# Making part of the low halves of split weights by an accumulating DMA in a two-layer decoder step

## The chip, the cores and the metric

The kernel runs on one core of one Trainium2 chip. The metric is the device time of one execution in microseconds, the median of several runs; lower is better.

## The reference, cut to what matters

The reference is one inference step of a two-layer decoder for 512 prompt tokens and 8 sample tokens that share the weights. Each layer is a half-step SwiGLU feed-forward network (FFN), a token mixer and a second FFN, each followed by a residual and a layernorm:

```python
def _swiglu(x, wg, wu, wd):
    return (jax.nn.silu(x @ wg) * (x @ wu)) @ wd

x = _layernorm(ALPHA * x + 0.5 * _swiglu(x, wg1, wu1, wd1), ...)
x = _layernorm(ALPHA * x + _mixer(x, ...), ...)
x = _layernorm(ALPHA * x + 0.5 * _swiglu(x, wg2, wu2, wd2), ...)
```

The model width is 1024, the FFN width 2816. The mixer has one input projection, three branches (windowed attention, a Mamba-2 scan, an HGRN2 scan), three gated branch projections and an output projection. All of it is float32. The multiplications by weights are most of the arithmetic, and the change concerns how a weight is made ready for them.

## The kernel before, in words

All 520 tokens stay on the chip, features on the 128 partitions and tokens along the free dimension, in two halves of 260 tokens. Weights are read from HBM in **units**. A float32 product is made of three matmuls in the type fp32r: a value is split into a high part (a copy rounded to fp32r) and a low part (the value less its high part), and `gemm` (lines 165 to 178) and `product` (lines 373 to 384) add high times high, weight high times activation low, and weight low times activation high, in this order.

The class `Weights` (from line 50) keeps the list of units in the order in which they are used. A **plain unit** is 128 rows by up to 1024 columns, mostly 512 KB (`_emit`, lines 77 to 92): SP loads it into a raw buffer `ws` (line 87), ScalarE copies it to `wh` (line 90), VectorE subtracts `wh` from `ws` into `wl` (line 91). A **pair** (`_emit_pair`, lines 94 to 113) is a gate unit g and an up unit u of an FFN, from which seven block products in the manner of Strassen are made in place of eight: sums of blocks are formed in two further raw buffers pa and pb by VectorE (L102, L103) and GpSimd (L104, L105), and `_split` (lines 67 to 75; cast L73, subtraction L74) splits g, pb, pa and the second half of u: seven quarters of 512 columns. There are five buffers each of `ws`, `wh` and `wl`, and a single one for the narrow split of u. `get` hands out the next unit and emits two units more than that; the emission has the highest priority (`EARLY[0]`), so a unit is loaded and split as soon as buffers allow.

TensorE uses most units for both token halves. At the end of an FFN or mixer the last projection is run over all units for the first half and then, with the same units loaded again, for the second half (`halves_last`), and the next stage begins likewise (`halves_head`, and the first ten projections of the mixer), so that the layernorm of one half (`ln_end`, lines 204 to 232, among it GpSimd's L224, VectorE's L225 and ScalarE's L228) runs beside matmuls of the other. A unit used for one half only is called a half unit below. Per layer there are 191 plain units (48 in each FFN, 95 in the mixer) and 36 pairs. An FFN has 16 half units at its start and 16 at its end, a mixer 20 and 16.

The order of instructions on each engine is fixed when the program is built: a scheduler with a timing model plays the program through and picks by priority. Each engine then runs its own list in order and waits on semaphores. All DMAs are issued by SP; GpSimd issues none.

Of the kernel before, what the change touches and what calls it, by code (L numbers as in the profile page):

```python
# [11 lines left out]
F32 = mybir.dt.float32  # L12
# [3 lines left out]
AF = mybir.ActivationFunctionType  # L16
ALU = mybir.AluOpType
# [32 lines left out]
class Weights:  # L50
# [13 lines left out]
    def _raw(self):  # L64
        return self.pool.tile([P, 1024], F32, tag="ws", name="ws", bufs=5)

    def _split(self, s, n=1024):
        nc = self.nc
        tag, bufs = ("", 5) if n > 512 else ("2", 1)
        h, lo = (  # L70
            self.pool.tile([P, 1024 if n > 512 else 512], F32R, tag=t + tag, name=t, bufs=bufs) for t in ("wh", "wl")
        )
        nc.scalar.copy(h[:, :n], s[:, :n])  # L73
        nc.vector.tensor_tensor(lo[:, :n], s[:, :n], h[:, :n].bitcast(F32), op=ALU.subtract)  # L74
        return h, lo

    def _emit(self):
        nc = self.nc
        unit = self.units[len(self.tiles)]
        with self.tc.high_priority(offset=EARLY[0]):  # L80
            if len(unit) == 2:
                self.tiles.append(self._emit_pair(*unit))
                return
            ap, kt, cols = unit
            n = kt * cols
            s = self._raw()
            nc.sync.dma_start(s[:, :n], ap)

            h, lo = (self.pool.tile([P, 1024], F32R, tag=t, name=t, bufs=5) for t in ("wh", "wl"))
            nc.scalar.copy(h[:, :n], s[:, :n])  # L90
            nc.vector.tensor_tensor(lo[:, :n], s[:, :n], h[:, :n].bitcast(F32), op=ALU.subtract)  # L91
        self.tiles.append((h, lo, kt, cols))

    def _emit_pair(self, ap0, ap1):


        nc = self.nc
        g, u, pa, pb = (self._raw() for _ in range(4))
        a, b = slice(0, 512), slice(512, 1024)
        nc.sync.dma_start(g, ap0)  # L100
        nc.sync.dma_start(u, ap1)
        nc.vector.tensor_tensor(pa[:, a], g[:, a], u[:, a], op=ALU.add)  # L102
        nc.vector.tensor_tensor(pb[:, a], pa[:, a], u[:, b], op=ALU.add)  # L103
        nc.gpsimd.tensor_tensor(pb[:, b], pb[:, a], g[:, b], op=ALU.add)  # L104
        nc.gpsimd.tensor_tensor(pa[:, b], u[:, a], u[:, b], op=ALU.add)  # L105
        gs, bs, as_ = self._split(g), self._split(pb), self._split(pa)
        us = self._split(u[:, b], 512)
        half = lambda t, k: tuple(x[:, k * 512 : k * 512 + 512] for x in t)
        return {
            "11": half(gs, 0), "21": half(gs, 1), "22": half(us, 0),  # L110
            "P1": half(as_, 0), "P3": half(as_, 1), "P2": half(bs, 0), "P4": half(bs, 1),
        }
# [1379 lines left out]
```

## Time and profile before

| | |
|---|---|
| median of 3 runs | 2638.61 us (2634.75 to 2639.36) |
| the profiled execution | 2647.04 us |
| its span, first to last instruction | 2645.2 us |
| mean granted TensorE clock | 0.986 of full speed |
| TensorE matmul busy | 97% |
| VectorE, ScalarE, GpSimd busy | 74%, 47%, 25% |
| moved by DMA | 318.17 MB |

In the rows below, PE is TensorE's matmuls and PEld its weight loads, DVE is VectorE, ACT ScalarE, POOL GpSimd, SP the engine that issues DMAs; a q behind an engine's name is its instruction queue. L91 is line 91 of the kernel. An entry like `wl<-ws,wh` names the tile that is written and those that are read.

### The profile page before, as it was taken

Reading aid. Unit: us, or ns where it says so; the run is one execution under the profiler, and the core shown is the slowest. Engines: PE = TensorE matmul, PEld = TensorE weight load, DVE = VectorE, ACT = ScalarE, POOL = GpSimd, SP = SyncE. Lnnn points to the kernel's source line nnn. Section 1 sums busy time; section 2 is a strip of 40 time slices with the busy share of each in tenths; the row PEclk is TensorE's granted clock in tenths of the full one; section 3 lists DMA queues with packets and bytes.
Section 4 is the critical chain, followed back from the end, with each engine's and each line's share of the span. In section 5 each row is a group of like instructions: output and inputs, shape, how many; then the busy total and the mean of one; then the engine's idle time right before and its main releaser. Section 6 shows DMA issues by size and latency. Waiting matters only on the chain.

```text
span 2645.2 us, 51891 instructions
## 1 busy us (share of the span) xinstructions
PE 2557.0 (97%) x20784; PEld 2486.7 (94%) x20784; DVE 1949.5 (74%) x3702; ACT 1250.3 (47%) x2358; POOL 667.8 (25%) x587
## 2 busy tenths in 40 slices
PE   8999999999899999999999999999998999999998
PEld 8999999898789999999989999999987899999997
DVE  8785888855485588868887868888544845988586
ACT  6342565543334473434663435754433344635355
POOL 2121243300033341212321122433000434312124
PEclk9999999999899999999999999999998999999999
DMA  6341457422442343232542414564224424332233
GB/s 206 109 131 62 143 165 218 142 67 77 86 137 90 114 150 99 92 114 81 189 132 86 136 65 148 185 191 137 81 73 75 144 83 134 122 112 92 101 115 126
DMA packets 159890, 318.17 MB, mean 120 GB/s; under 512 B 46788, under 2 KB 82340, under 8 KB 159648
## 3 DMA queue, kind: packets, MB, share of 16 engines
q1 hardware_dynamic: 159648, 314.86, 37.5%
q8 instruction: 163, 2.67, 0.4%
q14 instruction: 79, 0.65, 0.1%
HBM read 302.93 MB, written 11.88 MB: 119 GB/s over the span
## 4 chain that ended last, share of the span: by engine, by line
PE 70%; DVE 14%; DMA 8%; issue 3%; ACT 2%; POOL 2%; SPq 0%; ACTq 0%; POOLq 0%; DVEq 0%
PE g L176 14%; PE g L177 14%; PE g L178 14%; PE g L382 6%; PE g L384 6%; PE g L383 6%; DMA cb<-in_sconv 4%; DVE wl L91 3%; PE s L382 2%; PE s L383 2%; PE s L384 2%; DMA smp<-r8d 2%; DVE y L225 1%; PE s L1078 1%; DMA ws<-in_w_gu 1%
## 5 line engine op out<-in xcount | busy, mean ns | idle before, releaser
L176 PE MATMUL g<-xh,wh 128*128 128x260 f32 (+1 forms) x2336 | 676.6, 290 | 22.9 <-ACT cb L785 16.9
L178 PE MATMUL g<-xh,wl 128*128 128x260 f32 (+1 forms) x2336 | 674.6, 289 | 3.2 <-DVE wl L91 3.1
L177 PE MATMUL g<-xl,wh 128*128 128x260 f32 (+1 forms) x2336 | 674.6, 289 | 0.7 <-DVE xl L1356 0.7
L90 ACT CAST wh<-ws 128x1024 fp32r<-128x1024 f32 (+1 forms) x382 | 389.5, 1024 | 351.9 <-PE g L177 226.9
L91 DVE TENSOR_TENSOR wl<-ws,wh 128x1024 fp32r<-128x1024 f32 (+1 forms) x382 | 466.8, 1224 | 109.3 <-ACT wh L90 108.3
L176 PEld LDWEIGHTS g<-xh,wh 128*128 128x128 f32 (+1 forms) x2336 | 445.3, 191 | 34.8 <-ACT cb L785 18.7
L178 PEld LDWEIGHTS g<-xh,wl 128*128 128x128 f32 (+1 forms) x2336 | 444.9, 191 | 10.9 <-DVE wl L91 4.3
L177 PEld LDWEIGHTS g<-xl,wh 128*128 128x128 f32 (+1 forms) x2336 | 444.9, 190 | 8.7 <-issue 4.5
L73 ACT CAST wh<-ws 128x1024 fp32r<-128x1024 f32 (+1 forms) x288 | 265.3, 941 | 289.9 <-PE g L177 161.9
L178 PE MATMUL g<-hh,wl 128*128 128x260 f32 x1408 | 396.6, 283 | 0.0
L177 PE MATMUL g<-hl,wh 128*128 128x260 f32 x1408 | 395.9, 283 | 0.0
L176 PE MATMUL g<-hh,wh 128*128 128x260 f32 x1408 | 392.6, 283 | 1.5 <-DVE y L251 1.5
L74 DVE TENSOR_TENSOR wl<-ws,wh 128x1024 fp32r<-128x1024 f32 (+1 forms) x288 | 318.4, 1112 | 89.3 <-ACT wh L73 87.7
L105 POOL TENSOR_TENSOR ws<-ws 128x512 f32<-128x512 f32 x72 | 131.8, 1831 | 648.3 <-DMA ws<-in_w_gu 267.8
L176 PEld LDWEIGHTS g<-hh,wh 128*128 128x128 f32 x1408 | 263.4, 189 | 2.0 <-DVE y L251 1.9
L178 PEld LDWEIGHTS g<-hh,wl 128*128 128x128 f32 x1408 | 264.7, 188 | 0.2
L177 PEld LDWEIGHTS g<-hl,wh 128*128 128x128 f32 x1408 | 264.8, 188 | 0.1
L382 PE MATMUL g<-xh,wh 128*128 128x260 f32 x864 | 246.3, 286 | 2.0 <-ACT wh L73 1.6
L383 PE MATMUL g<-xl,wh 128*128 128x260 f32 x864 | 244.7, 284 | 0.0
L384 PE MATMUL g<-xh,wl 128*128 128x260 f32 x864 | 242.0, 283 | 0.0
L382 PEld LDWEIGHTS g<-xh,wh 128*128 128x128 f32 x864 | 163.9, 190 | 4.5 <-ACT wh L73 3.0
L382 PE MATMUL g<-sx,wh 128*128 128x260 f32 x576 | 163.7, 284 | 3.9 <-ACT wh L73 3.9
(404 smaller groups left out, 5701.3 us busy)
## 6 DMA issues: line engine op xcount, KB each, us to landing
ws<-in_w_gu SPq DMA_DIRECT2D x208, 512.0 KB, 3.3
ws<-in_w_in SPq DMA_DIRECT2D x132, 512.0 KB, 3.4
ws<-in_w_dn SPq DMA_DIRECT2D x96, 512.0 KB, 4.4
ws<-in_w_out SPq DMA_DIRECT2D x32, 512.0 KB, 3.9
ws<-in_w_dn SPq DMA_DIRECT2D x32, 384.0 KB, 3.1
smp<-r8d SPq DMA_DIRECT2D x48, 256.0 KB, 4.7
ws<-in_w_br SPq DMA_DIRECT2D x24, 512.0 KB, 4.5
smp<-in_hgr SPq DMA_DIRECT2D x16, 256.0 KB, 5.0
```

Of the source, the lines that this page charges most:

```text
L73: nc.scalar.copy(h[:, :n], s[:, :n])
L74: nc.vector.tensor_tensor(lo[:, :n], s[:, :n], h[:, :n].bitcast(F32), op=ALU.subtract)
L90: nc.scalar.copy(h[:, :n], s[:, :n])
L91: nc.vector.tensor_tensor(lo[:, :n], s[:, :n], h[:, :n].bitcast(F32), op=ALU.subtract)
L105: nc.gpsimd.tensor_tensor(pa[:, b], u[:, a], u[:, b], op=ALU.add)
L176: nc.tensor.matmul(out, lhsT=h[:, wc], rhs=xh[:, c0:c1], start=st, stop=False)
L177: nc.tensor.matmul(out, lhsT=h[:, wc], rhs=xl[:, c0:c1], start=False, stop=False)
L178: nc.tensor.matmul(out, lhsT=lo[:, wc], rhs=xh[:, c0:c1], start=False, stop=en)
L225: nc.vector.scalar_tensor_tensor(y, y, gn, rb, op0=ALU.mult, op1=ALU.mult)
L382: nc.tensor.matmul(out, lhsT=h[:, wc], rhs=xh, start=first and k == 0, stop=False, **go)
L383: nc.tensor.matmul(out, lhsT=h[:, wc], rhs=xl, start=False, stop=False, **go)
L384: nc.tensor.matmul(out, lhsT=lo[:, wc], rhs=xh, start=False, stop=k == HK - 1, **go)
```

## The change

A new helper `_parts` makes both parts of a split. With `dma` set, ScalarE still copies the high part and then writes the raw weights, negated and rounded to fp32r, into `lo`: the negated high part. GpSimd then issues a DMA that adds the raw weights to `lo`, which leaves the low part. Otherwise VectorE subtracts as before. The DMA is used for every second plain unit that is at least 512 columns wide, the first one included (the turn also passes at narrow units), and for g of each pair, two of its seven quarters. The sizes and numbers of buffers, the loads and the matmuls are the same.

```diff
--- before.py
+++ after.py
@@ -64,15 +64,24 @@
     def _raw(self):
         return self.pool.tile([P, 1024], F32, tag="ws", name="ws", bufs=5)
 
-    def _split(self, s, n=1024):
+    def _split(self, s, n=1024, dma=False):
+
         nc = self.nc
         tag, bufs = ("", 5) if n > 512 else ("2", 1)
         h, lo = (
             self.pool.tile([P, 1024 if n > 512 else 512], F32R, tag=t + tag, name=t, bufs=bufs) for t in ("wh", "wl")
         )
+        self._parts(h, lo, s, n, dma)
+        return h, lo
+
+    def _parts(self, h, lo, s, n, dma):
+        nc = self.nc
         nc.scalar.copy(h[:, :n], s[:, :n])
-        nc.vector.tensor_tensor(lo[:, :n], s[:, :n], h[:, :n].bitcast(F32), op=ALU.subtract)
-        return h, lo
+        if dma:
+            nc.scalar.activation(lo[:, :n], s[:, :n], AF.Copy, scale=-1.0)
+            nc.gpsimd.dma_start(lo[:, :n], s[:, :n], accum_op=ALU.add)
+        else:
+            nc.vector.tensor_tensor(lo[:, :n], s[:, :n], h[:, :n].bitcast(F32), op=ALU.subtract)
 
     def _emit(self):
         nc = self.nc
@@ -87,8 +96,8 @@
             nc.sync.dma_start(s[:, :n], ap)
 
             h, lo = (self.pool.tile([P, 1024], F32R, tag=t, name=t, bufs=5) for t in ("wh", "wl"))
-            nc.scalar.copy(h[:, :n], s[:, :n])
-            nc.vector.tensor_tensor(lo[:, :n], s[:, :n], h[:, :n].bitcast(F32), op=ALU.subtract)
+            self.turn = not getattr(self, "turn", False)
+            self._parts(h, lo, s, n, self.turn and n >= 512)
         self.tiles.append((h, lo, kt, cols))
 
     def _emit_pair(self, ap0, ap1):
@@ -103,7 +112,7 @@
         nc.vector.tensor_tensor(pb[:, a], pa[:, a], u[:, b], op=ALU.add)
         nc.gpsimd.tensor_tensor(pb[:, b], pb[:, a], g[:, b], op=ALU.add)
         nc.gpsimd.tensor_tensor(pa[:, b], u[:, a], u[:, b], op=ALU.add)
-        gs, bs, as_ = self._split(g), self._split(pb), self._split(pa)
+        gs, bs, as_ = self._split(g, dma=True), self._split(pb), self._split(pa)
         us = self._split(u[:, b], 512)
         half = lambda t, k: tuple(x[:, k * 512 : k * 512 + 512] for x in t)
         return {
```

## Rows read from the trace of the kernel before

**Rows 1.** The page, part 1: busy us, share of the span and instructions of each engine.
```profile
PE 2557.0 (97%) x20784; PEld 2486.7 (94%) x20784; DVE 1949.5 (74%) x3702; ACT 1250.3 (47%) x2358; POOL 667.8 (25%) x587
```

**Rows 2.** The page, part 4, by line: shares of the chain that ended last.
```profile
PE g L176 14%; PE g L177 14%; PE g L178 14%; PE g L382 6%; PE g L384 6%; PE g L383 6%; DMA cb<-in_sconv 4%; DVE wl L91 3%; PE s L382 2%; PE s L383 2%; PE s L384 2%; DMA smp<-r8d 2%; DVE y L225 1%; PE s L1078 1%; DMA ws<-in_w_gu 1%
```

**Rows 3.** Stretches of 53 us: us, busy (x instructions) by engine, PEclk, DMA share, GB/s.
```profile
0.00:53.00 53.00, 46.17 (x353) 45.28 (x354) 44.00 (x95) 37.48 (x68) 10.17 (x17) 1.00 0.68 236
...
371.00:424.00 53.00, 50.34 (x405) 49.70 (x404) 42.07 (x64) 38.21 (x64) 18.25 (x23) 0.97 0.56 184
...
954.00:1007.00 53.00, 48.10 (x379) 46.88 (x377) 48.69 (x85) 35.70 (x66) 17.13 (x17) 0.97 0.40 132
...
1007.00:1060.00 53.00, 52.86 (x426) 52.84 (x427) 43.64 (x73) 18.66 (x29) 8.75 (x6) 0.97 0.35 110
...
1272.00:1325.00 53.00, 51.59 (x427) 51.26 (x426) 45.81 (x69) 32.51 (x52) 24.29 (x22) 1.00 0.52 168
...
1325.00:1378.00 53.00, 48.64 (x391) 47.47 (x391) 49.12 (x83) 34.87 (x65) 16.07 (x16) 1.00 0.36 113
...
1643.00:1696.00 53.00, 50.47 (x415) 50.03 (x414) 45.85 (x66) 35.41 (x55) 27.10 (x26) 1.00 0.54 171
...
2226.00:2279.00 53.00, 50.40 (x401) 49.76 (x401) 43.74 (x65) 33.99 (x53) 30.13 (x28) 0.97 0.56 178
...
2279.00:2332.00 53.00, 50.75 (x406) 50.11 (x405) 49.59 (x83) 32.53 (x62) 13.15 (x11) 0.97 0.33 105
...
1166.00:1219.00 53.00, 53.00 (x445) 53.00 (x444) 31.66 (x49) 19.00 (x28) 9.73 (x7) 1.00 0.18 60
```

**Rows 4.** The same view of the four stretches with pairs.
```profile
106.00:318.00 212.00, 210.42 (x1744) 209.21 (x1743) 163.07 (x256) 89.91 (x145) 46.86 (x29) 1.00 0.30 98
...
1060.00:1272.00 212.00, 211.92 (x1760) 211.13 (x1759) 162.28 (x258) 91.57 (x148) 46.32 (x28) 1.00 0.32 108
...
1378.00:1643.00 265.00, 264.07 (x2192) 262.81 (x2191) 204.33 (x332) 110.25 (x176) 53.23 (x33) 1.00 0.34 112
...
2332.00:2597.00 265.00, 264.93 (x2201) 264.22 (x2200) 203.97 (x332) 111.34 (x179) 52.33 (x33) 1.00 0.33 108
```

**Rows 5.** Waits: idle us of the engine in total, times, longest us.
```profile
ACT wh L90 <- PE g L177: 226.9, 123, 6.2
```

**Rows 6.** Groups by line and shape: busy us, mean ns of one, idle before and its releasers.
```profile
L91 DVE TENSOR_TENSOR wl<-ws,wh 128x1024 fp32r<-128x1024 f32 x348 | 435.9, 1255 | 105.5 <-ACT wh L90 104.5
...
L74 DVE TENSOR_TENSOR wl<-ws,wh 128x1024 fp32r<-128x1024 f32 x216 | 264.4, 1226 | 74.2 <-ACT wh L73 72.6
...
L90 ACT CAST wh<-ws 128x1024 fp32r<-128x1024 f32 x348 | 362.7, 1046 | 303.6 <-PE g L177 209.9 <-PE g L383 37.8 <-issue 34.2
```

**Rows 7.** Line 105 alone: duration of one, ns, min/median/max.
```profile
L105 POOL TENSOR_TENSOR ws<-ws x72: 1280/1798/3575, 46.6 to 2565.7; 128x512 f32<-128x512 f32 x72
```

**Rows 8.** DMA queues and issues: share of 16 engines; count, KB, median us to landing.
```profile
q1 hardware_dynamic: 159648, 314.86, 37.5%
...
ws<-in_w_gu SPq DMA_DIRECT2D x208, 512.0 KB, 3.3
...
ws<-in_w_br SPq DMA_DIRECT2D x24, 512.0 KB, 4.5
...
smp<-in_hgr SPq DMA_DIRECT2D x16, 256.0 KB, 5.0
```

**Rows 9.** Timeline of one pair on ACT, POOL and SP: start us, us, instruction.
```profile
1228.35 1.05 ACT L73 CAST wh<-ws 128x1024 fp32r<-128x1024 f32 x1 [1.56 <-DMA ws<-in_w_gu]
...
1234.19 1.28 POOL L104 TENSOR_TENSOR ws<-ws 128x512 f32<-128x512 f32 x1 [2.39 <-DVE ws L103]
...
1235.51 0.33 SPq L100 DMA_DIRECT2D ws<-in_w_gu  x1
```

**Rows 10.** Timeline of the start on ACT and PE.
```profile
4.21 1.04 ACT L90 CAST wh<-ws 128x1024 fp32r<-128x1024 f32 x1 [2.20 <-DMA ws<-in_w_gu]
...
7.29 0.42 PE L178 MATMUL g<-xh,wl 128*128 128x260 f32 x1
```

## The prediction

> **What bounds the kernel now.** I read the page's engine busy times first: TensorE is busy for 97% of the span, VectorE for 74%, ScalarE for 47%, GpSimd for 25% [rows 1]. So the end is set by matmuls, and taking work from VectorE gains only where TensorE waits for it. The chain that ended last says how much that can be: matmuls fill it, and the subtraction of L91 holds 3% [rows 2], some 79 us of 2645.2, of which the change takes half at most.
>
> Where TensorE loses time is read from stretches of equal length [rows 3]. The stretch from 1166 us is a full one: 445 matmuls in 53 us, so a pitch of 0.119 us. The eight stretches listed at the ends of layers (last down projection, layernorm, first half units of the next stage) have 405, 379, 426, 427, 391, 415, 401 and 406: 310 too few, 36.9 us. In them VectorE is busy for 368.5 us of 424 (87%) and ScalarE for 261.9 (62%). In the four stretches with pairs [rows 4] 113 matmuls are missing of 954 us' worth, 13.5 us in all; there is little to win there.
>
> How early a weight unit is split follows from one wait: the cast of L90 sat idle 226.9 us, 123 times, until a matmul that read the high part had ended [rows 5]. The cast waits for one of five buffers, so the unit is made as soon as TensorE lets go of the unit five before: four units ahead. At the pitch above a half unit (24 matmuls) takes 2.86 us, a whole one 5.7 us, a pair (84 matmuls) 10.0 us. The lead is therefore 11.4 us among half units and 22.9 us among whole ones. There are 200 half units (32 in each of four FFNs, 36 in each of two mixers), in seven unbroken stretches.
>
> **The change, part by part.**
>
> *VectorE.* Of 382 plain units every second one moves; the two dt units are too narrow for it, and one of them has the turn, so 190 move, and with one a pair (72) that is 262 subtractions. At 1.255 and 1.226 us [rows 6] (16 of them are 768 wide and shorter) that is some 325 us less: 1949.5 becomes about 1625 us, 61%.
>
> *ScalarE.* 262 negated copies, bounded by the cast of the same shape at 1.046 us [rows 6], which is also the value I take: 274 us more, 1250 becomes 1524 us, 58%. In the eight stretches about half of some 115 plain units move: VectorE falls by about 70 us to 70%, ScalarE rises by 60 us to 76%. The fullest engine beside TensorE goes from 87% to 76%.
>
> *GpSimd.* 262 issues on its queue, which had no DMA. No row shows one. Below, nothing; above, 3.6 us, the longest of L105's additions; I take 1.3 us, the shortest of them [rows 7], since an issue moves no data through the engine. Each issue waits for the negated copy, and behind it stand L104, L105, and in a layernorm the subtractions of L224.
>
> *The DMAs.* No row shows one that reads and adds to what is there. Loads of 512 KB land 3.3 to 4.5 us after their issue, and one of 256 KB takes 5.0 [rows 8]. A load occupies the 16 engines for 37.5% of 2645.2 us over 314.86 MB, times 0.524 MB: 1.65 us [rows 8]. The accumulating one has to read twice as much, so I take 4.5 + 1.65, about 6 us; the ends are 3.3 us, as a plain load, and 10 us, as two slow transfers one after the other. By the Trainium skill, "DMA: Bandwidth & Descriptors", Anatomy of one DMA, a GpSimd-issued transfer takes 2.0 us plus its bytes at 436 GB/s; an estimate from that is 3.2 us, or 4.4 us with the second read, and with it the sum below would be about 3 us better, as no half unit would be late; no row here shows such a transfer.
>
> *The path of a moved unit.* Cast 1.05, negated copy 1.05, issue 1.3, landing 6: 9.4 us from the start of the cast, against 2.3 us and VectorE's queue now. Whole units have 22.9 us, so nothing is lost there. Half units have 11.4 us; 2.0 are to spare, and ScalarE's own queue takes some of that. I take +3 us over the seven stretches; the ends are 0 and, with a landing of 10 us, 2.0 us late. Every late unit holds up the next, so the lateness comes back once in six units (five for the buffer, one for the turn): 33 times 2.0, +67 us.
>
> *The eight stretches.* TensorE lost 36.9 us there. I take half of that back, -18 us, because the other half is the layernorm's own chain through all engines, which no load on VectorE explains. The ends are 0 and -25 us.
>
> *Pairs.* Only g moves, which is split before u has landed. Its cast begins at 1228.35, so its low part would be there at 1237.75 us. Until now g's raw buffer was last read by L104, ending at 1235.47, and SP issued the next g load at 1235.51 [rows 9]: that load goes out up to 2.2 us later, with u's load behind it on SP's queue. Against that stands 1.23 us taken from VectorE's queue in front of L102 and L103, which are next to be late. Net 1.0 us per pair at worst, and only once the stock of split weights is used up, near the end of a group of eight. I take +2 us for eight groups; the ends are -5 and +72 us (all 72 pairs).
>
> *Start.* The first unit of all has the turn: cast at about 4.2 us, low part at 13.6, and the first matmul with it now runs at 7.29 [rows 10]. That is 6.3 us late, less what can be run of other units' high parts meanwhile: +3 us, ends 0 and +6.3.
>
> *The convolution loads* in the mixer, 4% of the chain [rows 2], share the DMA engines: the added transfers occupy them for some 262 times 2 to 3.3 us, 20 to 33% more. Of this +1 us, ends 0 and +10.
>
> **The sum:** 3 - 18 + 2 + 3 + 1 = -9 us. The profiled execution took 2647.04 us (span 2645.2 and 1.8 around it), 8.4 us over the median of the runs, 2638.61; the difference is carried over to the median: 2630 us. About 5 us (0.2%) is what a measurement of this kernel can tell from no change.
>
> **Rivals.**
>
> *The transfer is too late among half units* (slower). The place is the first matmul with wl in the half-unit stretches, the price 33 us for each microsecond by which the path passes 11.4 us, and it decides from a landing of 8 us. For it: DMA engines are already busy for 0.33 to 0.68 of the time there [rows 3], and each half unit brings a load of its own. Against it: the loads there land in 3.3 to 4.5 us all the same. With a landing of 9 us to 9.5 us, 33 to 50 us late and 18 us gained: 2654 to 2671 us. Chance 0.27.
>
> *GpSimd becomes the queue that everything stands in* (slower). L105 takes 1.28 us alone and 1.80 in the median, 3.58 at most [rows 7]: GpSimd's work is stretched while VectorE runs. With issues of 3.6 us the path is 11.7 us, 0.3 late (10 us), and in each of six layer ends one issue stands in front of L224 (22 us); less 18 us gained that is +14: 2653 us. Chance 0.10. The Trainium skill, "SBUF — State Buffer", Who interferes with whom, has such a rule: GpSimd cannot write descriptors while VectorE runs in a two-port mode; it also says that two-input operations, which most here are, have no such mode.
>
> *Gain and loss cancel* (no change): if what TensorE loses at the layer ends is mostly the layernorm's chain, the relief gives 5 to 10 us and the other terms take 9: 2638 to 2643 us, about 2640. The chain's 3% for L91 speaks against it, the few waits of TensorE itself that end with wl for it. The order of all instructions is planned anew, which alone can move some microseconds either way. Chance 0.18. That the change does not do what it says I give nothing: the high part subtracted and the raw part added are the same numbers.
>
> **How the numbers follow.** The forecast's own case, relief worth more than lateness, has 0.45, with 2608 to 2633 us as its range. The slower cases have 0.37, the even one 0.18. The range goes from 2608 (25 us of relief and 5 in the pairs) to 2685 us, where a landing of almost 10 us ends less the relief; outside are the pairs' worst end and anything beyond.
>
> **What would show it.** L91 should stand at 192 and L74 at 216, a ScalarE group of 262 copies should appear, and 262 issues on GpSimd's queue with 5 to 7 us to landing. VectorE should fall to about 1625 us and ScalarE rise to about 1525. The eight stretches should hold some 150 matmuls more. The forecast is wrong if TensorE's waits name a DMA into wl among half units, if GpSimd's issues take 3 us or more, or if the pair stretches lose more than they do now.

## The result, and where the time went

The changed kernel takes 2919.67 us (median, 2915.28 to 2926.39) against 2638.99 us before: a ratio of 1.1069, 95% interval 1.1045 to 1.1094, so some 281 us slower. The profiled execution has a span of 2924.6 us. Its page, parts 1, 3, 5 and 6, with the lines that answer to [rows 1, 6, 8]:

```profile
span 2924.6 us, 52737 instructions
...
PE 2647.9 (91%) x20784; PEld 2552.3 (87%) x20784; DVE 1656.0 (57%) x3440; ACT 1481.4 (51%) x2620; POOL 801.1 (27%) x849
...
q1 hardware_dynamic: 159648, 314.86, 33.8%
q0 software_dynamic: 37728, 135.28, 24.4%
...
L187 PE MATMUL g<-xh,wl 128*128 128x260 f32 (+1 forms) x2336 | 694.6, 298 | 65.4 <-DMA wl<-ws 65.2
...
L84 DVE TENSOR_TENSOR wl<-ws,wh 128x1024 fp32r<-128x1024 f32 (+2 forms) x408 | 474.4, 1163 | 285.9 <-ACT wh L79 279.0
L82 POOL DMA_DIRECT2D wl<-ws x262 | 231.7, 884 | 1290.7 <-ACT wl L81 324.8
...
L187 PE MATMUL g<-hh,wl 128*128 128x260 f32 x1408 | 404.0, 289 | 45.3 <-DMA wl<-ws 45.3
...
L81 ACT ACTIVATE wl<-ws 128x1024 fp32r<-128x1024 f32 (+1 forms) x262 | 272.7, 1041 | 0.1
...
wl<-ws POOLq DMA_DIRECT2D x246, 512.0 KB, 5.6
ws<-in_w_gu SPq DMA_DIRECT2D x208, 512.0 KB, 3.8
ws<-in_w_in SPq DMA_DIRECT2D x132, 512.0 KB, 5.6
```

The line numbers of the changed kernel are about nine higher: L79 is the cast, L81 the negated copy, L82 the DMA, L84 the subtraction, L187 the third matmul of `gemm`. VectorE was relieved nearly as forecast (1949.5 to 1656.0 us), ScalarE's copies cost what was forecast, and the new transfers land in 5.6 us in the median of all; among half units it is 8.2 us at the heads and ends of the FFNs and 8.5 us at the heads of the mixers. (Head is the run of half units at the start of an FFN or mixer, end the run at its end.) Yet TensorE, busy for 97% before, is at 91%, and its waits name the transfer:

```profile
PEld g L187 <- DMA wl<-ws: 134.2, 68, 6.2
...
PE g L187 <- DMA wl<-ws: 120.0, 63, 5.9
```

(the view of the waits: us in all, times, longest). Two stretches of 53 us among half units, the first layernorm and the mixer's head behind it, to be read against 445 matmuls in a full one [rows 3]:

```profile
364.00:417.00 53.00, 40.03 (x304) 38.46 (x305) 24.84 (x42) 30.04 (x45) 18.97 (x24) 0.94 0.75 187
417.00:470.00 53.00, 41.73 (x304) 40.44 (x303) 23.75 (x40) 33.70 (x52) 15.73 (x20) 0.90 0.73 184
```

141 matmuls are missing in each, a third, and VectorE (the third busy time of a row) is busy for less than half of the time: it is no longer what TensorE waits for.

The units come in the same order in both kernels, so the stretch of a group of units, from its first matmul to that of the next group, can be compared group by group. The table gives the change of each kind against before, in us of the profiled executions, for the changed kernel and for five of the experiments below: ring1536 (that many bytes for DMA descriptors), nohalf, ringnopair, copy512 and actonly. The last matmuls of a group of pairs and the first of the down projection behind it stand mixed, not alike in all kernels; a stretch begins here with the first matmul of its own kind, so up to 9 us can stand in one row that belong to the next.

| stretches | changed | 1536 | no half units moved | 1536, no g moved | DMA copies, does not add | no DMA at all |
|---|---|---|---|---|---|---|
| half units, heads of FFNs | +63 | +28 | +3 | +27 | +10 | -12 |
| half units, ends of FFNs | +67 | +36 | +2 | +22 | +1 | 0 |
| half units, mixers | +73 | +5 | +3 | +10 | -3 | -5 |
| eight groups of eight pairs | +40 | +56 | +62 | +3 | +1 | -7 |
| whole units, mixers | +21 | +16 | +7 | +21 | -12 | -24 |
| all else in the FFNs | +15 | +22 | +21 | +13 | -2 | -1 |
| sum | +279 | +163 | +98 | +96 | -5 | -49 |

**One at a time.** The timeline of the changed kernel shows how the half units were lost. The negated copies on ScalarE, and the issues on GpSimd's queue, among half units (start us, us, instruction):

```profile
373.12 1.06 ACT L81 ACTIVATE wl<-ws 128x1024 fp32r<-128x1024 f32 x1
...
378.65 1.06 ACT L81 ACTIVATE wl<-ws 128x1024 fp32r<-128x1024 f32 x1
...
386.85 1.05 ACT L81 ACTIVATE wl<-ws 128x1024 fp32r<-128x1024 f32 x1
```

```profile
372.52 0.89 POOL L82 DMA_DIRECT2D wl<-ws  x1
...
382.06 0.88 POOL L82 DMA_DIRECT2D wl<-ws  x1 [7.88 <-issue]
...
392.09 0.89 POOL L82 DMA_DIRECT2D wl<-ws  x1 [7.54 <-issue]
...
400.51 0.89 POOL L82 DMA_DIRECT2D wl<-ws  x1 [5.93 <-DVE ht L209]
```

The copy that ends at 374.2 us has its transfer issued at 382.1, the next (379.7) at 392.1, the third (387.9) at 400.5. GpSimd was idle before them, and at two of the three the profile finds nothing that it waited for ("issue"). The transfers issued at 372.5, 382.1 and 392.1 landed at 381.7, 391.8 and 400.2 by their semaphores: each issue begins 0.3 us after the landing of the one before. That is so for 91 of the 262 issues, and none of the 262 begins before the last one has landed. A round takes 8 to 10 us where two half units give 5.7.

### The profile page after: what moved, and what is told of

Same layout as the page of the kernel before. It is cut to its first block, busy times and chain, and to the rows that moved or that the text cites. A ratio compares the mean times of both kernels' runs of the same rounds, so it can differ in the third digit from the quotient of the medians.

```text
span 2924.6 us, 52737 instructions
## 1 busy us (share of the span) xinstructions
PE 2647.9 (91%) x20784; PEld 2552.3 (87%) x20784; DVE 1656.0 (57%) x3440; ACT 1481.4 (51%) x2620; POOL 801.1 (27%) x849
## 3 DMA queue, kind: packets, MB, share of 16 engines
q0 software_dynamic: 37728, 135.28, 24.4%
## 5 line engine op out<-in xcount | busy, mean ns | idle before, releaser
L79 ACT CAST wh<-ws 128x1024 fp32r<-128x1024 f32 (+2 forms) x670 | 655.9, 987 | 919.8 <-PE g L186 363.6
L187 PE MATMUL g<-xh,wl 128*128 128x260 f32 (+1 forms) x2336 | 694.6, 298 | 65.4 <-DMA wl<-ws 65.2
L185 PE MATMUL g<-xh,wh 128*128 128x260 f32 (+1 forms) x2336 | 691.0, 296 | 39.2 <-ACT cb L794 21.4
L84 DVE TENSOR_TENSOR wl<-ws,wh 128x1024 fp32r<-128x1024 f32 (+2 forms) x408 | 474.4, 1163 | 285.9 <-ACT wh L79 279.0
L82 POOL DMA_DIRECT2D wl<-ws x262 | 231.7, 884 | 1290.7 <-ACT wl L81 324.8
L187 PEld LDWEIGHTS g<-xh,wl 128*128 128x128 f32 (+1 forms) x2336 | 461.7, 198 | 80.6 <-DMA wl<-ws 73.3
L185 PEld LDWEIGHTS g<-xh,wh 128*128 128x128 f32 (+1 forms) x2336 | 462.2, 198 | 49.8 <-ACT cb L794 22.8
L186 PEld LDWEIGHTS g<-xl,wh 128*128 128x128 f32 (+1 forms) x2336 | 461.6, 198 | 9.4 <-issue 4.5
L187 PE MATMUL g<-hh,wl 128*128 128x260 f32 x1408 | 404.0, 289 | 45.3 <-DMA wl<-ws 45.3
L187 PEld LDWEIGHTS g<-hh,wl 128*128 128x128 f32 x1408 | 270.3, 192 | 50.7 <-DMA wl<-ws 50.5
L81 ACT ACTIVATE wl<-ws 128x1024 fp32r<-128x1024 f32 (+1 forms) x262 | 272.7, 1041 | 0.1
L114 POOL TENSOR_TENSOR ws<-ws 128x512 f32<-128x512 f32 x72 | 122.5, 1702 | 464.8 <-DMA ws<-in_w_gu 425.3
L393 PEld LDWEIGHTS g<-xh,wl 128*128 128x128 f32 x864 | 163.5, 189 | 28.4 <-DMA wl<-ws 27.6
L391 PE MATMUL s<-sx,wh 128*128 128x260 f32 x576 | 166.7, 289 | 19.4 <-DVE ht L425 19.4
```

The source lines that it names most:

```text
L81: nc.scalar.activation(lo[:, :n], s[:, :n], AF.Copy, scale=-1.0)
L82: nc.gpsimd.dma_start(lo[:, :n], s[:, :n], accum_op=ALU.add)
L185: nc.tensor.matmul(out, lhsT=h[:, wc], rhs=xh[:, c0:c1], start=st, stop=False)
L186: nc.tensor.matmul(out, lhsT=h[:, wc], rhs=xl[:, c0:c1], start=False, stop=False)
L187: nc.tensor.matmul(out, lhsT=lo[:, wc], rhs=xh[:, c0:c1], start=False, stop=en)
L391: nc.tensor.matmul(out, lhsT=h[:, wc], rhs=xh, start=first and k == 0, stop=False, **go)
```

## The experiments

Times are medians; the ratios are to the kernel before, measured beside each, with 95% intervals.

**How many at a time: ring1024, ring1536, once512; and nohalf.**

The first three put the tiles btok and cbm into the set `ONCE`, which gives them one buffer; the space is 1024, 1536 and 512 bytes. In the fourth, half is set for the half units.

```diff
-    nc = _bacc.Bacc("TRN2", target_bir_lowering=False, num_devices=1, dynamic_dma_scratch_size=512)
+    nc = _bacc.Bacc("TRN2", target_bir_lowering=False, num_devices=1, dynamic_dma_scratch_size=1024)
```

```diff
-            self._parts(h, lo, s, n, self.turn and n >= 512)
+            self._parts(h, lo, s, n, self.turn and n >= 512 and not half)
```

> The changed kernel with the space for GpSimd's DMA descriptors doubled, from 512 to 1024 bytes per partition; to make room, two small tiles of the mixer (btok and cbm) have one buffer instead of two. Theory A (one transfer at a time: in the changed kernel 90 of 261 issues begin 0.3 us after the landing of the one before, though cast, load and negated copy were ready up to 12 us earlier): two transfers can be under way, those 90 issues follow their negated copy, and most of the 281 us goes: 2640 to 2700 us. Theory B (the transfer itself is too slow beside the loads: it lands after 8.3 us where the loads are dense and after 4.7 us elsewhere, and the units follow from that): the issues come earlier but land later, the time stays within 2880 to 2930 us.

> The same with 1536 bytes, three times the space. Theory A: as with 1024 or a little better (0 to 20 us less), because among half units a moved unit is due every 5.7 us and a transfer beside loads takes 6 to 8 us, so two under way nearly suffice. Theory B: 2880 to 2930 us.

> The changed kernel with the two small tiles in one buffer each, and the descriptor space left at 512 bytes: instruction for instruction the kernel of the two runs above. It shows what the two tiles cost. Both theories: 2910 to 2935 us, as the changed kernel, since the mixer that uses them lost nothing there.

> The changed kernel, but every half unit is subtracted by VectorE as before; of the whole plain units every second one, and of each pair g, still go through the DMA. Theory A and theory B alike put the loss into the half units: what is left is some 4 to 5 us for each of the eight groups of pairs, 30 to 40 us: 2665 to 2685 us. A third theory, C (it is the 1.05 us negated copies on ScalarE or the 0.9 us issues on GpSimd that hold up the stages everywhere): the loss falls only with the number of moved units, 100 of 262, so to some 2810 us.

Measured: 1024 bytes 2802.98 us (1.0596 to 1.0631), 1536 bytes 2804.74 us (1.0588 to 1.0644), 512 bytes with the same instructions 2945.41 us (1.1135 to 1.1170), no half units 2743.06 us (1.0362 to 1.0400). The two tiles cost 26 us that were not expected, and the descriptor space alone is worth 142 us. With 1024 bytes 58 issues begin while the transfer before is under way, and 3 instead of 89 (the run with 512 bytes and the same tiles) sit at a landing: theory A's mechanism is shown, and theory B falls. From 364 to 440 us, GpSimd's idle time before the issues that nothing in the profile explains ("issue"), the waits of TensorE's weight loads for the transfer (us, times) and the landings were these in the changed kernel; with 1024 bytes, in the second block, there is no such idle time:

```profile
  issue: 31.5, 4
...
  PEld g L187: 12.6, 7
...
DMA to landing us min/median/max: 5.7/8.4/9.7
```

```profile
  PEld g L187: 4.7, 4
...
DMA to landing us min/median/max: 5.2/7.3/10.4
```

But the 2640 to 2700 us that theory A promised were not reached; 160 us stay, and 1536 bytes are no better than 1024. Without moved half units 100 us stay, where theories A and B had 30 to 40 and theory C 170: the groups of pairs cost 62 us there. Why they cost only 40 us in the changed kernel is not shown.

**The price of each part: relief, actonly, ringnopair, dmaonly.**

```diff
 # relief: no low part for the moved tiles
-            nc.scalar.activation(lo[:, :n], s[:, :n], AF.Copy, scale=-1.0)
-            nc.gpsimd.dma_start(lo[:, :n], s[:, :n], accum_op=ALU.add)
+            return h
 # actonly: the copy without the DMA
-            nc.gpsimd.dma_start(lo[:, :n], s[:, :n], accum_op=ALU.add)
 # ringnopair: 1536 bytes
-        gs, bs, as_ = self._split(g, dma=True), self._split(pb), self._split(pa)
+        gs, bs, as_ = self._split(g), self._split(pb), self._split(pa)
 # dmaonly: 1536 bytes, a plain DMA without the copy
-            nc.scalar.activation(lo[:, :n], s[:, :n], AF.Copy, scale=-1.0)
-            nc.gpsimd.dma_start(lo[:, :n], s[:, :n], accum_op=ALU.add)
+            nc.gpsimd.dma_start(lo[:, :n], s[:, :n].bitcast(F32R))
```

> What the relief of VectorE is worth when nothing is paid for it: the moved units and quarters have no low part at all (no negated copy, no DMA, no subtraction); the third matmul of each set reads the high part a second time. It leaves out the low parts of those 262 tiles. Theory D (the prediction's term of -18 us was right, VectorE's load makes TensorE wait at the layer ends): 2612 to 2628 us. Theory E (TensorE's missing matmuls there are the layernorm's own chain, and less load on VectorE brings nothing; in the run with 1536 bytes the stretches of half units in the mixer and its output lost nothing, yet gained nothing either): 2633 to 2645 us.

> The changed kernel without its 262 DMAs: the negated copy stays and is what the third matmul reads. It leaves out the addition of the raw weights. It prices ScalarE's part with VectorE's relief. If ScalarE's 1.05 us copies are hidden, as the prediction had it, the time is that of the run without any low part, within 5 us. If they stand in front of casts and layernorm steps and hold them up: 2660 to 2720 us, most of it in the half units at the heads and ends of the feed-forward stages, where 65 us are left of the loss with the larger descriptor space.

> The run with 1536 bytes, but g of each pair is subtracted by VectorE again, so 190 units are moved instead of 262. In the runs with 1024 and 1536 bytes and in that without moved half units alike, the eight groups of eight pairs last 55 to 62 us longer than before. If that is the price of g's transfer (it holds the raw buffer, so the next pair's loads start later), the time falls by 50 to 65 us, to 2740 to 2755 us. If the groups are late for another reason (VectorE or ScalarE in front of them), it falls by less than 20 us.

> The run with 1536 bytes without its 262 negated copies: a plain DMA on GpSimd's queue copies the raw weights into the low tile. It leaves out the subtraction of the high part, so the third matmul reads the raw weights. It prices transfer and issue without ScalarE's part, and with one read a row instead of two. If the transfer is what is left of the loss: 2720 to 2800 us. If it is the chain of cast, negated copy and transfer together, in which the copy takes 1 us of the lead: 2680 to 2720 us.

Measured: 2593.73 us (0.9822 to 0.9853), 2599.56 us (0.9843 to 0.9874), 2743.53 us (1.0369 to 1.0420) and 2623.64 us (0.9934 to 0.9965). The relief is worth 44 us when nothing is paid for it, more than either theory had; the page says where TensorE stands then:

```profile
PE 2530.2 (98%) x20784; PEld 2469.1 (95%) x20784; DVE 1623.1 (63%) x3440; ACT 1247.0 (48%) x2358; POOL 620.7 (24%) x587
```

Twenty-four of the 49 us in the table's last column are in the mixers' whole units, where the prediction did not look; of its eight stretches the heads of the FFNs and mixers give 17. ScalarE's 262 copies cost 6 us: hidden, nearly as forecast. g costs 61 us, the groups of pairs falling from +56 to +3. And a plain DMA in place of copy and adding DMA leaves 30 us of loss against no low part at all, where 86 or more were expected: neither the issue on GpSimd nor a transfer as such is what hurts most.

**Adding against copying: plainchain, copy512, plain512, negfirst.**

```diff
 # plainchain (1536 bytes) and copy512 (the changed kernel as it stands)
-            nc.gpsimd.dma_start(lo[:, :n], s[:, :n], accum_op=ALU.add)
+            nc.gpsimd.dma_start(lo[:, :n], s[:, :n].bitcast(F32R))
 # plain512: dmaonly with 512 bytes and the changed kernel's tiles
 # negfirst (1536 bytes): the cast moves behind the DMA
-        nc.scalar.copy(h[:, :n], s[:, :n])
         if dma:
             nc.scalar.activation(lo[:, :n], s[:, :n], AF.Copy, scale=-1.0)
             nc.gpsimd.dma_start(lo[:, :n], s[:, :n], accum_op=ALU.add)
-        else:
+        nc.scalar.copy(h[:, :n], s[:, :n])
+        if not dma:
```

> The run with 1536 bytes, negated copies and all, but the DMA that follows each copy only copies the raw weights over it instead of adding them: one read a row, same place in the order. It leaves out the addition. It tells what the 181 us between that run (2805 us) and the one with a plain DMA and no copy in front (2624 us) are. Theory F (the adding transfer itself: its packets take 2.7 us of 16 engines against 1.4 us for a plain one, and beside two loads of 1.65 us each pair of half units asks 6.0 us of the engines in 5.7 us): 2630 to 2670 us. Theory G (the place in the order: the transfer may begin only after cast and negated copy, and holds the raw buffer until it lands): 2750 to 2805 us.

> The changed kernel as it stands, 512 bytes and all, with its 262 transfers copying the raw weights instead of adding them. It leaves out the addition. The run with a plain DMA and no copy in front did not notice the smaller space (2627 us with 512 bytes, 2624 with 1536), and the one with the copy in front took 2646 us with 1536. Theory L (the adding transfer alone, by its longer time on the engines and by filling the descriptor space): 2630 to 2655 us, so some 270 of the 281 us hang on that word. Theory M (with 512 bytes plain transfers behind negated copies come in bunches and go one at a time as well): 2670 to 2750 us.

> The run with a plain DMA and no copy in front, with the descriptor space and the tiles of the changed kernel (512 bytes). It leaves out the subtraction. It tells whether the space holds up plain transfers as it does adding ones. If a plain transfer also fills the space (one at a time): 2640 to 2680 us, with issues 0.3 us after the landing of the one before. If a plain one, with half the reads, leaves room for a second: within 10 us of 2624 us.

> The run with 1536 bytes with the negated copy ahead of the cast: ScalarE writes the negated rounded weights from the raw ones first, the DMA is issued, and the high part is cast while it runs. Nothing is left out. Theory G: the path is 1.05 us shorter for every moved unit, and the raw buffers come free as much earlier, which takes 40 to 90 us off 2805 us: 2715 to 2765 us. Theory F: the engines are no less busy, at most 25 us less: 2780 to 2805 us.

Measured: 2646.49 us (1.0010 to 1.0041), 2650.64 us (1.0024 to 1.0065), 2626.78 us (0.9933 to 0.9970), 2816.40 us (1.0627 to 1.0694). Theories F and L hold, G and M fall: with `accum_op` gone, and all copies, issues, waits and the small space in place, 269 of the 281 us are gone, and a path shorter by a microsecond with the adding left in gains nothing (2816 us is 11 us beyond theory F's range, on the slow side). The plain transfer with 512 bytes is within 10 us of 2624, so it did not go one at a time. One thing is not kept apart: the copying transfers name their source as fp32r, the adding one reads it as float32 into an fp32r tile, and no run adds without this change of type. The same queue and group of the copying kernel (copy512), parts 3, 5 and 6 of its page:

```profile
q0 software_dynamic: 37728, 135.28, 14.4%
...
L82 POOL DMA_DIRECT2D wl<-ws x262 | 147.0, 561 | 1064.8 <-ACT wl L81 386.7
...
wl<-ws POOLq DMA_DIRECT2D x246, 512.0 KB, 3.4
```

TensorE's matmuls of L187 wait for the transfer for 8.1 us there, against 120.0 us in the changed kernel. For the same packets and bytes the adding queue took 24.4% of 16 engines over 2924.6 us, 2.72 us a transfer; the copying one takes 14.4% over 2640.6 us, 1.45 us. A transfer with no load beside it lands after 4.6 us (median) when it adds and 2.9 us when it copies; the issue takes 0.88 and 0.56 us of GpSimd. And copying ones are not held to one at a time by 512 bytes: 31 issues begin before the landing of the one before, three sit at it.

**Fewer, smaller, or on another engine: fourth, halfcols, pool4.**

```diff
 # fourth (no g moved)
-            self._parts(h, lo, s, n, self.turn and n >= 512)
+            self._parts(h, lo, s, n, self.turn % 4 == 0 and n >= 512)
 # halfcols (no g moved), m = n // 2
-            nc.scalar.activation(lo[:, :n], s[:, :n], AF.Copy, scale=-1.0)
-            nc.gpsimd.dma_start(lo[:, :n], s[:, :n], accum_op=ALU.add)
+            nc.scalar.activation(lo[:, m:n], s[:, m:n], AF.Copy, scale=-1.0)
+            nc.gpsimd.dma_start(lo[:, m:n], s[:, m:n], accum_op=ALU.add)
+            nc.vector.tensor_tensor(lo[:, :m], s[:, :m], h[:, :m].bitcast(F32), op=ALU.subtract)
 # pool4: as fourth, with GpSimd subtracting
+            nc.gpsimd.tensor_tensor(lo[:, :n], s[:, :n], h[:, :n].bitcast(F32), op=ALU.subtract)
```

> The changed kernel (512 bytes) with every fourth plain unit moved instead of every second, and no quarter of a pair: 95 adding transfers instead of 262, each as long as before. Among half units the engines are then asked for 9.4 us in 11.4 us (four loads of 1.65 us and one transfer of 2.76 us), and a transfer has 11.4 us to land before the next is issued, so the descriptor space holds nothing up. Theory H (the engines' time decides): nothing is lost among half units and about a third of the relief's 44 us is gained: 2622 to 2638 us. Theory I (the landing decides: 8 us beside loads, after cast and copy, is more than the lead): every moved half unit is still late, some 50 of them at 0.3 to 0.6 us: 2645 to 2670 us.

> The changed kernel (512 bytes) with every second plain unit moved, but only the second half of its columns: ScalarE copies and the DMA adds 512 columns, VectorE subtracts the other 512; no quarter of a pair. 190 adding transfers of 256 KB. The engines are asked for some 4.7 us in 5.7 us, and the transfer lands sooner by about 1.4 us. Theory H: as with every fourth unit, 2622 to 2638 us. Theory I: less late than there, 2630 to 2650 us. If the descriptor space still holds them up one by one (128 rows each, as before), the transfers queue among half units: 2680 to 2750 us.

> Every fourth plain unit's low part is subtracted by GpSimd instead of VectorE; no negated copy, no DMA, no quarter of a pair. If GpSimd does 1024 columns in 3 to 4 us beside VectorE, the path is 5 us and fits every lead: about a third of the 44 us is gained, 2622 to 2638 us. If GpSimd's queue (the layernorm's subtractions stand behind it, in the mixer the whole state work) or a slower VectorE beside it eats that: 2640 to 2665 us.

Measured: 2668.22 us (1.0088 to 1.0120), 2750.44 us (1.0395 to 1.0428), 2688.61 us (1.0170 to 1.0203). Every fourth unit still loses 21 us at the heads and ends of the FFNs while the mixers gain 5: theory I, the landing, decides there, though the engines are not full: TensorE waits for the transfer 20.8 us in all, in 14 longer waits and not in some 50 short ones. Half the columns come out at the upper end of the last case of their forecast: 60 issues sit at the landing before, none begins ahead of it, so it is not the bytes of a transfer that fill the space. Of the 111 us that this kernel loses, TensorE's waits name the transfer for 19.5; the rest is not explained. GpSimd as the subtractor missed both of its ranges; its page says why:

```profile
PE 2570.6 (96%) x20784; PEld 2499.4 (93%) x20784; DVE 1965.9 (73%) x3607; ACT 1251.0 (47%) x2360; POOL 906.4 (34%) x682
...
L81 POOL TENSOR_TENSOR wl<-ws,wh 128x1024 fp32r<-128x1024 f32 (+1 forms) x95 | 243.0, 2558 | 725.1 <-ACT wh L79 635.4
```

VectorE lost 95 subtractions, some 119 us at 1.255 us [rows 6], and is busy for 16 us more than before [rows 1]: the rest of its work takes some 135 us longer.

**The loop of a pair, and the mixers alone: nohalf_add, mix4.** In the run without moved half units, in the middle of a group of eight pairs (ScalarE, GpSimd, SP):

```profile
1267.48 1.05 ACT L79 CAST wh<-ws 128x1024 fp32r<-128x1024 f32 x1 [2.13 <-DMA ws<-in_w_gu]
1268.43 1.05 ACT L81 ACTIVATE wl<-ws 128x1024 fp32r<-128x1024 f32 x1
```

```profile
1268.75 1.77 POOL L114 TENSOR_TENSOR ws<-ws 128x512 f32<-128x512 f32 x1 [7.80 <-DMA ws<-in_w_gu]
1270.46 0.88 POOL L82 DMA_DIRECT2D wl<-ws  x1
```

```profile
1251.89 0.33 SPq L109 DMA_DIRECT2D ws<-in_w_gu  x1
...
1263.55 0.33 SPq L109 DMA_DIRECT2D ws<-in_w_gu  x1
...
1276.97 0.33 SPq L109 DMA_DIRECT2D ws<-in_w_gu  x1
...
1288.39 0.33 SPq L109 DMA_DIRECT2D ws<-in_w_gu  x1
...
1300.14 0.33 SPq L109 DMA_DIRECT2D ws<-in_w_gu  x1
```

It reads as a closed loop through g's raw buffer: load, cast, negated copy, then the issue behind the addition L114 that waits for u, then the landing, which lets the next load of g go. The loads of g are 12.1 us apart in the mean of these four rounds (the 13.4 us in the expectation below is the longest), where the matmuls of a pair take 10.0 us.

```diff
 # nohalf_add
-        nc.gpsimd.tensor_tensor(pa[:, b], u[:, a], u[:, b], op=ALU.add)
+        nc.vector.tensor_tensor(pa[:, b], u[:, a], u[:, b], op=ALU.add)
 # mix4 (no g moved; mix is set for the mixer's input and branch units)
-            self._parts(h, lo, s, n, self.turn and n >= 512)
+            self._parts(h, lo, s, n, mix and self.turn % 4 == 0)
```

> The run without moved half units, with one addition of each pair (the second half of pa, on L114) made by VectorE instead of GpSimd, so that the issue for g no longer stands behind an addition that waits for u's load. There, in the middle of a group of eight, g's loads go out 13.4 us apart: 3.9 us from load to cast, 0.95 to the negated copy, 2.0 behind L114, 6.2 to the landing, 0.3 to the next load. Theory J (the loop through g's raw buffer, GpSimd's queue being 2 us of it): the loads come about 11.4 us apart, the groups of eight lose 10 to 30 us instead of 62, and the time falls from 2743 us to 2685 to 2715 us. Theory K (the transfer's landing decides, or VectorE's extra 0.7 us a pair eats it): above 2730 us.

> The changed kernel (512 bytes) with every fourth unit of the mixers moved and nothing else: no unit of the feed-forward stages, none of the output projection, no quarter of a pair; 38 or so transfers. In the run with every fourth unit everywhere the mixers' stretches were together 5 us shorter than before and the heads and ends of the feed-forward stages 21 us longer. If that holds when the latter are left alone: 2630 to 2636 us, 3 to 9 us faster than before. If moving so little changes nothing: 2636 to 2642 us.

Measured: 2708.30 us (1.0236 to 1.0281) and 2645.37 us (0.9999 to 1.0021). Theory J holds: with the addition off GpSimd's queue the loads of g follow each other every 10.9 us.

```profile
1226.88 0.33 SPq L109 DMA_DIRECT2D ws<-in_w_gu  x1
...
1238.24 0.33 SPq L109 DMA_DIRECT2D ws<-in_w_gu  x1
...
1249.25 0.33 SPq L109 DMA_DIRECT2D ws<-in_w_gu  x1
...
1259.78 0.33 SPq L109 DMA_DIRECT2D ws<-in_w_gu  x1
...
1270.66 0.33 SPq L109 DMA_DIRECT2D ws<-in_w_gu  x1
```

In this kernel two matmuls of the down projections stand 48 and 58 places earlier among those of the pairs, so the table's way of cutting stretches would show the pairs too short and what follows too long. Cut by the number of matmuls instead, the groups of eight fall from +65 to +26 us, within theory J's 10 to 30, and the ends of the FFNs stay at +1. The last run is a miss: the mixers alone give nothing that can be told from no change, though every fourth unit everywhere had shown 5 us there. No kernel of the study that computes all of the low parts is faster than the one before.

## Why the prediction was wrong, step by step

The change did what the first steps said. The counts and durations of the moved work came out: 262 copies at 1.041 us (1.046 taken), issues of 0.88 us (1.3 taken), 5.6 us to landing over all transfers (6 taken; but 8.2 to 8.5 us at the heads and ends of the FFNs and the heads of the mixers, where it counted), VectorE at 1656 us (1625), ScalarE at 1481 us (1524). The sign named beforehand, a wait of TensorE for a DMA into wl among half units, is the one that appeared. It was the first rival that came true, at four to six times its price.

**The step that failed first is the path of a moved unit:** "cast 1.05, negated copy 1.05, issue 1.3, landing 6: 9.4 us", with an issue that waits for the negated copy alone. The table gives the medians from the start of the cast to the landing for moved half units, and, in the last column, the lead that the kernel before gave its half units, from cast to first matmul with the low part:

| half units | changed | 1536 | 1536, DMA copies | lead before |
|---|---|---|---|---|
| heads of FFNs | 14.1 | 9.7 | 7.8 | 9.6 |
| ends of FFNs | 13.9 | 10.4 | 8.3 | 9.9 |
| heads of mixers | 18.2 | 9.5 | 8.3 | 11.6 |
| output projections | 11.4 | 8.5 | 6.3 | 11.7 |

The term that rests on this path was +3 us; the moved half units' stretches lost 203 us. With space for more than one transfer the path is what was forecast, 8.5 to 10.4 us. With 512 bytes it is 3 to 9 us longer, by a wait that belongs to no instruction. I had bounded the issue (0 to 3.6 us) and the landing (3.3 to 10 us) each by itself, as if a second transfer could always go out beside the first; the allocation, `dynamic_dma_scratch_size=512` where the program is built, was not asked how many it holds.

**"Half units have 11.4 us; 2.0 are to spare"** is the second. Worked out from matmul times, it is right in the mixers (11.6 and 11.7 us) and 1.5 to 1.8 us too long at the heads and ends of the FFNs. There a cast starts 2.8 and 1.7 us (medians, kernel before) after the last matmul on its buffer, while ScalarE does other casts, the layernorm's steps and, at the heads, the splits of the activations' sums; in the mixers it is 1.2 and 0.1 us. At the FFNs 64 us are left with 1536 bytes, while the mixers' half units lose 5: where the path of 9.5 us fits the lead, almost nothing is lost.

**"The lateness comes back once in six units"** is the third, the price of the rival. One at a time, a transfer cannot catch up: of 100 moved half units some 75 were used within 0.6 us of their landing, and their stretches lost 203 us, 2.0 us for every moved one, instead of 33 times the lateness.

**The pairs** were taken at +2 us with an end at +72. Alone they cost 61 us (ringnopair against ring1536) and 62 us (nohalf's groups of eight). "Net 1.0 us per pair at worst" was the right size for a pair (62 us over 64); what failed is "only once the stock of split weights is used up". The loads of g were 11.4 us apart already before (median of the last five gaps of each group), more than the 10.0 us of a pair's matmuls, so there was little to spare; that each microsecond of the loop is then paid at each pair is argued from this and from nohalf_add (11.8 us with g moved, 11.0 with the addition on VectorE). The forecast also missed the place in GpSimd's queue: the issue comes 1.0 us after the copy, behind L114.

**The relief** was taken at -18 us and measures -44 us without a price. The mechanism was right; the term was too small, because only the ends of stages were listed and not the mixers' branches. **The convolution loads** (+1 us) stand in the same branches: what is gained there without a DMA (-24 us) is turned into +21 us. TensorE's waits for the convolution's tile cb rise only from 16.9 to 21.4 us, so most of that has another cause, which is not shown. **The start** (+3 us) is part of the FFN heads: the first of them alone loses 23 us.

**GpSimd's queue** as the rival had it, 3.6 us an issue, did not come: with 1536 bytes the issue follows the copy by 0.4 us in the median at all half units.

**The clock** was in no term. Matmuls are busy for 90.9 us more than before [rows 1], a third of the loss. The mean granted clock fell from 0.986 to 0.959 of 2.4 GHz; 241 us of the span are at 1.2 GHz instead of 77 us, the rest at 2.4 GHz. It falls in stretches in which TensorE has just been waiting (0.90 and 0.94 in the two windows above, 1.00 in [rows 3]'s full one), so a wait costs more than its own length.

The ladder in the changed kernel's own setting: 2639 before; 2594 with the relief alone; 2600 with ScalarE's copies; 2651 with transfers that copy (without the copy in front it is 2627 us, so of these 51 us some 18 are the later start behind cast and copy: 24 less ScalarE's 6); 2920 when they add. Open is how the 158 us that adding costs with space enough divide between the engines' time and the later landing. Every fourth unit shows that landing matters with the engines at leisure; with every second, two loads of 1.65 us and one adding transfer of 2.72 us ask for 6.0 us of the 16 engines in 5.7 us, by estimate.

## What to carry to other kernels

A transfer that replaces an engine's work has a number of places beside its duration: ask how many can be under way at once, from the space that holds their descriptors, and look for issues that begin a fixed moment after the landing of the one before. Read the lead of a buffer from the trace, from making to first use in each stage, not from the pitch of its consumer, and where a stage's loads already follow from one another through a buffer, count every microsecond of the new path at each round. Price a relief by leaving the work out before looking for a cheaper place for it: here 44 us were to be had, and no kernel that still computes all of the low parts kept any of them.

## What the runs showed of the hardware that was not expected

- An adding transfer of 128 rows of 4096 bytes moves its packets of 4096 bytes in 342 ns each, a copying one in 181 ns: 1.89 times. The Trainium skill, "Collectives: The Full Stack", The bandwidth ceiling, puts a reducing transfer's lower rate down to its two source reads, not to the addition, and gives a measured ratio of 1.93. The ratio here is near it; the trace does not show the reads themselves.
- With 512 bytes of descriptor space one adding transfer is under way, whatever the columns (512 columns each: still none of 190 issues ahead of a landing), and two copying ones can be; with 1024 bytes three adding ones were, four times. The Trainium skill, "DMA: Bandwidth & Descriptors", Terms and The descriptor swizzle, has 16 bytes for a descriptor and nine reading ones per engine for a transfer to 128 partitions; nine packets per engine agree with the page (37728 packets, 262 transfers, 16 engines). An estimate from these two is 144 bytes for a copying transfer and, with two reads a row, 272 for an adding one: three and one in 512 bytes, where no more than two copying ones were seen. No run here counts the descriptors themselves.
- An adding transfer alone lands after 4.6 us, a copying one after 2.9 us, near the 4.4 and 3.2 us that the prediction worked out as estimates. Where loads hold 40 to 60% of the engines (73 transfers of the changed kernel) the first packet of an adding transfer starts 4.7 us after the issue instead of 1.45 us, and it lands after 8.3 us (medians).
- GpSimd's subtraction of 128x1024 took 2.56 us, and with 95 of them VectorE's remaining work took some 135 us longer.
